# Two weight rings whose shifted blocks get columns of their own, and three small index tables that move

## The chip, the cores and the metric

The kernel runs on one core of one Trainium2 chip. The metric is the time of one execution in device microseconds (us). Before the change it was measured three times: 1804.21, 1804.41 and 1804.79 us, with a median of 1804.41 us.

## What is computed

The reference is a two-layer encoder trunk for one sequence of 256 tokens with 1024 features. Each layer is a token mixer and a channel mixer, each followed by a residual sum and a layer norm.

```python
for i in range(2):
    m = mla(x) if i == 0 else dsa(x)             # token mixer
    x = layernorm(alpha * x + m)
    x = layernorm(alpha * x + peer(x))           # channel mixer

# dsa (layer 1): h = x @ w_in gives q, k, v (8 heads of 128), index queries (8 heads of 64),
# one index key of 64 and 8 index weights for each token
score = sum_h w_idx[:, h] * relu(q_idx[:, h] @ k_idx.T)     # chunk-causal
sel   = top_k(score, 64)                                    # 64 keys for each query
o     = softmax(q @ k[sel].T * scale) @ v[sel];   m = o @ w_o

# peer: q = x @ w_q, two sub-keys for each head, top 16 x top 16 -> 16 of 16384 experts for each head
a = x @ w_down.T;  y = (gelu(a) * gate) @ w_up
```

The kernel computes all 16384 experts of a layer densely (128 blocks of 128 experts) and multiplies by a gate matrix that is zero for the experts that weren't chosen.

## The kernel before, in words

**The weights as a stream of blocks.** Nearly all weights pass through one object, `Stream` (L55 to L140). A block is 128 partitions by 1024 columns of float32. Its life has four steps. `_load` (L81) issues the DMA from HBM into one of four `raw` buffers, on the SP queue. `_split` (L99) lets ScalarE round it to a shorter format (`hi`, L106) and VectorE, at times GpSimd, subtract to get what is left (`lo`, L110 or L108). Then TensorE multiplies: each product is the sum of three, hi by hi, hi by lo and lo by hi, and all matmuls of the projections are issued in L264. `get()` (L114) hands out block i and, before it returns, issues the splits up to block i + 3 (`AHEAD`, L58) and the loads up to i + 6.

**The rings.** The `hi` and the `lo` parts have a buffer each (`ring`, L221): 4 slots of 1024 columns and 64 columns of padding. `parts(i)` (L75) places block i in slot i % 4. A block that TensorE streams as the moving operand (`moving=True` in L222 to L240) starts at the slot's first column; a block whose slices are loaded as stationary weights starts 16 columns later (`SKEW`). A shifted block therefore reaches 16 columns into the next slot. Between blocks of one kind this costs nothing, as all are shifted alike. Where the kind changes, a shifted block and the unshifted block in the next slot share 16 columns, and the instructions that write and read these columns are ordered by semaphores, in program order.

**The blocks by number**, in the order of the `add` calls: 0 to 5 `mla_h` and 6 to 12 `mla_qk` (shifted); 13 and 14 `mla_v`, 15 to 22 `mla_w_o`, 23 to 26 the first of `peer_q` (moving); 27 to 38 the rest of `peer_q` and 39 to 166 `down` (shifted); 167 to 294 `up` and 295 to 298 the first of `dsa_v` (moving); 299 to 302 `dsa_iq` and 303 `dsa_ik` (shifted); 304 to 307 the rest of `dsa_v` (moving); 308 to 323 `dsa_qk` (shifted); 324 to 331 `dsa_w_o` and 332 to 335 `peer_q` (moving); 336 to 347 `peer_q` and 348 to 475 `down` (shifted); 476 to 603 `up` (moving).

**The stage of the second half of `dsa_v`.** In `dsa()` the loop of L893 runs over the blocks 304 to 307, that is over c = 4 to 7, and for each over the two token tiles t. `rows` (L300) issues six matmuls of 512 columns for one block and one tile: two by each of hi, lo and hi again. Between them stand `weigh()` (L852: two small transposes of the index weights, PSUM tile `wi`) after block 305's first tile, and then `pick(2)`, which issues the index scores of two heads (PSUM tile `il`, L864). All of these matmuls are linked in program order by `pe()` (L254, from L891 on). The index key that `il` needs comes out of block 303 by a chain of copies and multiplications on ScalarE and VectorE: L845 and L846 (ScalarE), L847 to L849 (VectorE), L850 (ScalarE, the key's second copy) and L851 (ScalarE, the index weights). Behind the loop come the queries `q` from block 308 on.

Since `get()` splits three blocks ahead, `get()` for block 305 issues the split of block 308, the first shifted block, ahead of block 305's `rows`; block 306's call issues the split of 309, and block 307's that of 310.

**The start.** GpSimd writes `iota` (the numbers 0 to 127), VectorE casts it to `iota16` (L215) and, spread out, to `iotac` (L217), and GpSimd to `iota4` (L216). `first()` (L1198) begins with dummy matmuls (`busy`, L1204), which have `iota16` as weights and `iotac` as moving operand, until the first inputs are there.

**The order of instructions** that the program leaves open on ScalarE, VectorE and GpSimd is drawn up when the kernel is built, from a list of dependences and estimated times.

Of the kernel before, what the change touches and what calls it, by code (L numbers as in the profile page):

```python
# [10 lines left out]
F32 = mybir.dt.float32  # L11
F32R = mybir.dt.float32r
F16 = mybir.dt.float16
# [5 lines left out]
P = 128  # L19
T = 256  # L20
D = 1024
# [26 lines left out]
GSCALE = 2.0 ** 14  # L48
RING = 4
SKEW = 16  # L50
DSA_POOL = 3
MAGIC = 12582912.0


class Stream:  # L55
# [18 lines left out]

    def parts(self, i):  # L75

        skew = 0 if self.moving[i] else SKEW
        at = i % RING * D + skew
        return [ring[:, at : at + self.blocks[i][1]] for ring in (self.hi, self.lo)]

    def _load(self, upto):  # L81
# [89 lines left out]
def tile_trunk(ctx: ExitStack, tc: tile.TileContext, ins, out: bass.AP):  # L171
    nc = tc.nc
    def pool(name, bufs, **kw):
        return ctx.enter_context(tc.tile_pool(name=name, bufs=bufs, **kw))

    lead = pool("lead", 1)
    wide = pool("wide", 1)
    raws = pool("raws", 4)
    rings = pool("rings", 1)
    big = pool("big", 1)  # L180
    const = pool("const", 1)
# [9 lines left out]
    def ps(name):  # L191
        return psp.tile([P, 512], F32, tag="ps", name=name)
# [2 lines left out]
        return pyp.tile([P, 512], F32, tag=f"py{i}", name=name)  # L195

    ident = lead.tile([P, P], F32, tag="ident", name="ident")
    iota = const.tile([P, P], F32, tag="iota", name="iota")
    ones = lead.tile([P, 16], F32, tag="ones", name="ones")[:, 0:1]
    mhalf = lead.tile([P, 16], F32, tag="mhalf", name="mhalf")[:, 0:1]  # L200
    keep = [dram.tile([P, D], F32, tag=f"x{t}", name=f"x{t}") for t in range(2)]
    xh = wide.tile([P, NC, T], F32R, tag="xh", name="xh")
    xl = wide.tile([P, NC, T], F32R, tag="xl", name="xl")
    place16 = const.tile([P, 2, T], F16, tag="place16", name="place16")
    gate16 = const.tile([P, T], F16, tag="gate16", name="gate16")
    rest = const.tile([P, T], F32, tag="rest", name="rest")
    iota16 = lead.tile([P, P], F16, tag="iota16", name="iota16")
    iota4 = const.tile([P, P, 4], F16, tag="iota4", name="iota4")
    iotac = const.tile([P, CELLS, TOPK], F16, tag="iotac", name="iotac")
    arena = big.tile([P, 32768], F32, tag="arena", name="arena")  # L210
    A = arena.rearrange("p (b t) -> p b t", t=T)

    make_identity(nc, ident)
    nc.gpsimd.iota(iota, pattern=[[1, P]], base=0, channel_multiplier=0, allow_small_or_imprecise_dtypes=True)
    nc.vector.tensor_copy(iota16, iota)  # L215
    nc.gpsimd.tensor_copy(iota4, iota[:, :, None].to_broadcast([P, P, 4]))  # L216
    nc.vector.tensor_copy(iotac, iota[:, :CELLS, None].to_broadcast([P, CELLS, TOPK]))  # L217
    nc.vector.memset(ones, 1.0)
    nc.vector.memset(mhalf, -0.5)

    ring = [rings.tile([P, RING * D + 64], F32R, tag=k, name=k) for k in ("hi", "lo")]  # L221
    ws = Stream(nc, raws, *ring)  # L222
    ws.add(ins["mla_h"][0:6])
    ws.add(ins["mla_qk"])
# [38 lines left out]
    def mm(o, l, r, start, stop):  # L263
        return pe(lambda: nc.tensor.matmul(o, l, r, start=start, stop=stop, skip_group_check=True))  # L264
# [48 lines left out]
    def queue_of():  # L313

        last = {}

        def queue(engine, emit):
            with ExitStack() as order:
                if engine in last:
                    order.enter_context(tc.issue_after(last[engine]))  # L320
                ins = emit()
            last[engine] = ins.ins
            return ins

        return queue
# [492 lines left out]
    def dsa():  # L818
# [82 lines left out]
        for t in range(2):  # L901
            for n in range(2):
                nc.scalar.copy(v[:, t, n * 512 : (n + 1) * 512], v4[t][n])
        ws.share = DSA_POOL
        for h in range(0, HEADS, 2):
# [22 lines left out]
    def peer(li):  # L928
# [186 lines left out]
        def place(g4, done):  # L1115
# [8 lines left out]
            if done < P:  # L1124
                nc.scalar.mul(A[:, done:, tsl], pv[:, done:, :], 1.0 / GSCALE)
            if done:
                nc.vector.scalar_tensor_tensor(A[:, :done, tsl], pv[:, :done, :], 1.0 / GSCALE, A[:, :done, tsl],
                                               op0=ALU.mult, op1=ALU.mult)
# [3 lines left out]
        for b0 in range(0, NKEYS, 2):  # L1132
# [9 lines left out]
            if t0 < T:  # L1142
                nc.scalar.activation(A[:, b0 : b0 + 2, t0:], pv[:, :, t0:], AF.Gelu)
            if t0 > 0:
                nc.scalar.activation(pv[:, :, :t0], pv[:, :, :t0], AF.Gelu)
                nc.vector.tensor_tensor(A[:, b0 : b0 + 2, :t0], A[:, b0 : b0 + 2, :t0], pv[:, :, :t0], op=ALU.mult)
            while groups < prepared:
# [16 lines left out]
        def operand(k):  # L1164
            if k % 2 == 0 and k not in parts:
                a = A[:, k : k + 2, :]
                slot = slice(k % NC, k % NC + 2)
# [30 lines left out]
    def first(o):  # L1198

        queue = queue_of()  # L1200
        idle = ps("idle")
        some = iotac.rearrange("p c k -> p (c k)")

        def busy(n, w=P):  # L1204
            for _ in range(n):
                queue("pe", lambda: nc.tensor.matmul(idle[:, :w], iota16, some[:, :w], start=True, stop=True))

        def x_high(c, engine="act"):
            emit = nc.scalar.copy if engine == "act" else nc.vector.tensor_copy
            queue(engine, lambda: emit(xh[:, piece[c], :], xt[:, piece[c], :]))  # L1210

        def x_low(c, engine="dve"):
            eng = nc.vector if engine == "dve" else nc.gpsimd
            return queue(engine, lambda: eng.tensor_tensor(xl[:, piece[c], :], xt[:, piece[c], :],
                                                           xh[:, piece[c], :].bitcast(F32), op=ALU.subtract))

        def w_low(i):
            s = slice(512 * i, 512 * i + 512)
            queue("dve", lambda: nc.vector.tensor_tensor(lo0[:, s], raw0[:, s], hi0[:, s].bitcast(F32),
                                                         op=ALU.subtract))  # L1220

        def passes(w, x, *pieces):
            for c in pieces:
                for k in (2 * c, 2 * c + 1):
                    queue("pe", lambda: mm(o, w[:, k * P : (k + 1) * P], x[:, k, :], k == 0 and w is hi0 and x is xh,
                                           k == NC - 1 and w is lo0))

        queue("act", lambda: nc.scalar.copy(hi0, raw0))
        x_high(0, "dve")
        x_high(1)  # L1230
        x_low(0)
        x_low(1)
        x_high(2)
        pooled = x_low(2, "pool")
        x_high(3)
        w_low(0)
        x_low(3)
        w_low(1)
        busy(WARM, 512)
        passes(hi0, xh, 0, 1)  # L1240
        busy(2)
        passes(hi0, xl, 0)
        passes(hi0, xh, 2)
        passes(hi0, xl, 1)
        passes(hi0, xh, 3)
        busy(2)
        passes(lo0, xh, 0, 1)
        passes(hi0, xl, 2, 3)
        passes(lo0, xh, 2, 3)
        return pooled  # L1250
# [78 lines left out]
```

## Time and profile before

| | |
|---|---|
| median of three runs | 1804.41 us |
| the profiled execution's own time | 1804.73 us |
| its span in the profile | 1803.0 us |
| TensorE (PE) busy | 1786.7 us |
| VectorE (DVE) busy | 1338.9 us |
| ScalarE (ACT) busy | 1054.0 us |
| GpSimd (POOL) busy | 404.4 us |
| granted TensorE clock, mean | 0.998 |

PE is TensorE's matmuls, PEld its weight loads, SPq the queue that issues most DMAs. In a row of the timeline stand the start in us from the span's beginning, the duration in us, the engine, the line, the operation, the tile written and the tiles read, the count, and in square brackets the engine's idle time ahead of it with what ended it. In a row of the waits stand the instruction that waited and what it waited for, then the total in us, the number of waits and the longest one. In a row of the chain of waits stand the start, the duration and what ran. In a row of the windows stand, for a stretch, each engine's busy time and its count of instructions, then the granted TensorE clock, the DMA share and GB/s.

### The profile page before, as it was taken

The numbers are of one execution on the slowest core, as the hardware profiler recorded it, in microseconds if no ns is written. First come the engines' busy times: TensorE is split into PE (matmuls) and PEld (weight loads), VectorE is DVE, ScalarE is ACT, GpSimd is POOL, SyncE is SP. The second block draws the span as 40 slices with busy tenths as digits, with TensorE's granted clock in tenths as the row PEclk, the third lists the DMA queues.
The fourth block names the chain that finished last, engine by engine and source line by source line (L and its number), as shares of the span: only waits on it lengthen the run. The fifth ranks groups of instructions, "written<-read, shape, count | busy, mean of one in ns | idle before, by whom it ended". The sixth has DMA issues, their size and how long they took to land.

```text
span 1803.0 us, 32368 instructions
## 1 busy us (share of the span) xinstructions
PE 1786.7 (99%) x12495; PEld 1632.4 (91%) x12495; DVE 1338.9 (74%) x2320; ACT 1054.0 (58%) x1832; POOL 404.4 (22%) x287
## 2 busy tenths in 40 slices
PE   9999999999999999999989999999999999999998
PEld 8899999999998888888879899999999988888886
DVE  6688998888985555555679789997889865555555
ACT  6655545888864444444556554557888754444443
POOL 2012354555520000000013013543555400000000
PEclk9999999999999999999999999999999999999999
DMA  7555566444456666666646555655444575666653
GB/s 244 199 176 176 190 199 197 159 159 163 164 197 216 194 195 191 197 190 196 209 133 220 180 170 181 202 193 175 165 164 165 167 239 190 196 191 195 192 193 118
DMA packets 93468, 335.47 MB, mean 186 GB/s; under 512 B 10368, under 2 KB 11392, under 8 KB 93312
## 3 DMA queue, kind: packets, MB, share of 16 engines
q1 hardware_dynamic: 93024, 332.87, 56.4%
q8 instruction: 98, 1.61, 0.3%
q14 instruction: 58, 0.48, 0.1%
q10 hardware_dynamic: 288, 0.52, 0.1%
HBM read 329.16 MB, written 4.19 MB: 185 GB/s over the span
## 4 chain that ended last, share of the span: by engine, by line
PE 98%; DVE 1%; issue 1%; ACT 0%; DMA 0%; SPq 0%; DVEq 0%; POOLq 0%; POOL 0%; ACTq 0%
PE y L264 41%; PE d L264 39%; PE pq L264 4%; PE G L264 3%; PE q L264 3%; PE v L264 2%; PE qw L264 1%; PE s L264 1%; PE ps L264 1%; PE h L264 1%; PE qi L264 1%; PE o L264 1%; PE qn L264 0%; DMA arena<-in_xT 0%; PE kn L264 0%
## 5 line engine op out<-in xcount | busy, mean ns | idle before, releaser
L110 DVE TENSOR_TENSOR lo<-raw,hi 128x1024 fp32r<-128x1024 f32 (+1 forms) x557 | 750.7, 1349 | 291.2 <-ACT hi L106 289.5
L106 ACT CAST hi<-raw 128x1024 fp32r<-128x1024 f32 (+1 forms) x583 | 611.0, 1049 | 525.1 <-PE d L264 222.9
L264 PE MATMUL d<-xh,hi 128*128 128x256 f32 x2048 | 572.9, 280 | 0.0
L264 PE MATMUL d<-xh,lo 128*128 128x256 f32 x2048 | 566.8, 277 | 0.0
L264 PE MATMUL d<-xl,hi 128*128 128x256 f32 x2048 | 566.8, 277 | 0.0
L264 PEld LDWEIGHTS d<-xh,lo 128*128 128x128 f32 x2048 | 385.1, 188 | 0.0
L264 PEld LDWEIGHTS d<-xh,hi 128*128 128x128 f32 x2048 | 384.8, 188 | 0.0
L264 PEld LDWEIGHTS d<-xl,hi 128*128 128x128 f32 x2048 | 384.7, 188 | 0.0
L264 PE MATMUL y<-hi,xh 128*128 128x512 f32 x1088 | 337.8, 390 | 0.0
L264 PE MATMUL y<-lo,xh 128*128 128x512 f32 x1088 | 337.6, 389 | 0.0
L264 PE MATMUL y<-hi,xl 128*128 128x512 f32 x1088 | 337.4, 389 | 0.0
L1108 POOL TENSOR_TENSOR gate<-hot,gate 128x512 f16<-128x512 f16 x128 | 220.5, 1741 | 214.3 <-DVE hot L1106 214.3
L264 PEld LDWEIGHTS y<-lo,xh 128*128 128x128 f32 x1088 | 204.1, 188 | 42.7 <-DVE lo L110 0.3
L264 PEld LDWEIGHTS y<-hi,xl 128*128 128x128 f32 x1088 | 204.2, 188 | 42.4
L264 PEld LDWEIGHTS y<-hi,xh 128*128 128x128 f32 x1088 | 203.8, 188 | 42.0
L358 POOL TENSOR_TENSOR st<-st,mhalf 128x1 f32<-128x1 f32 x8 | 4.4, 552 | 800.6 <-DVE st L356 800.6
L1112 ACT ACTIVATE gate<-hot,rest 128x128 f16<-128x128 f16 x512 | 165.8, 411 | 1.1 <-DVE hot L1106 1.0
L1169 ACT CAST xh<-arena 128x512 fp32r<-128x512 f32 x128 | 79.7, 623 | 145.5 <-PE y L264 145.4
L1170 DVE TENSOR_TENSOR xl<-arena,xh 128x512 fp32r<-128x512 f32 x128 | 88.2, 691 | 73.8 <-ACT xh L1169 73.8
L108 POOL TENSOR_TENSOR lo<-raw,hi 128x1024 fp32r<-128x1024 f32 x26 | 62.8, 2414 | 223.8 <-ACT hi L106 223.8
L1106 DVE TENSOR_TENSOR hot<-iota,place 128x1024 f16<-128x1024 f16 x128 | 85.6, 709 | 32.4 <-PE G L264 32.2
L1030 POOL TENSOR_TENSOR arena<-arena 128x800 f32<-128x800 f16 x32 | 71.0, 2229 | 58.0 <-DVE arena L1027 58.0
(220 smaller groups left out, 1805.7 us busy)
## 6 DMA issues: line engine op xcount, KB each, us to landing
raw<-in_down SPq DMA_DIRECT2D x256, 512.0 KB, 3.3
raw<-in_up SPq DMA_DIRECT2D x256, 512.0 KB, 4.3
raw<-in_peer_q SPq DMA_DIRECT2D x24, 512.0 KB, 5.0
raw<-in_dsa_qk SPq DMA_DIRECT2D x16, 512.0 KB, 3.3
raw<-in_mla_w_o SPq DMA_DIRECT2D x8, 512.0 KB, 5.3
arena<-in_peer_q SPq DMA_DIRECT2D x8, 512.0 KB, 4.2
raw<-in_dsa_v SPq DMA_DIRECT2D x8, 512.0 KB, 4.4
raw<-in_dsa_w_o SPq DMA_DIRECT2D x8, 512.0 KB, 3.4
```

Source lines behind the costliest of these rows:

```text
L106: self.act(lambda: nc.scalar.copy(hi, raw))
L108: nc.gpsimd.tensor_tensor(lo, raw, hi.bitcast(F32), op=ALU.subtract)
L110: self.dve(lambda: nc.vector.tensor_tensor(lo, raw, hi.bitcast(F32), op=ALU.subtract))
L264: return pe(lambda: nc.tensor.matmul(o, l, r, start=start, stop=stop, skip_group_check=True))
L358: nc.gpsimd.tensor_tensor(st[:, 5:6], st[:, 4:5], mhalf, op=ALU.pow)
L1030: nc.gpsimd.tensor_tensor(o.rearrange("p k c -> p c k"), same, cell[t][:, h, :, None].to_broadcast([P, CELLS, TOPK]), op=ALU.mult)
L1106: nc.vector.tensor_tensor(hot, iota4[:, None].to_broadcast([P, 2, P, 4]), place16[:, :, None, four].to_broadcast([P, 2, P, 4]), op=ALU.is_ ...
L1108: nc.gpsimd.tensor_tensor(gate[:, 0], hot[:, 1].rearrange("p c j -> p j c"), gate16[:, four, None].to_broadcast([P, 4, P]), op=ALU.mult)
L1112: nc.scalar.mul(gate[:, 1, j, :], hot[:, 1, :, j], rest[:, t : t + 1])
L1169: nc.scalar.copy(hh, a)
L1170: nc.vector.tensor_tensor(al, a, hh.bitcast(F32), op=ALU.subtract)
```

## The change

The rings become two pairs of slots of 2112 columns each (`PAIR`), 4224 columns in place of 4160. In a pair, the even slot's block starts at column 0 (moving) or 16 (shifted), and the odd slot's block at 1088 (moving) or 1040 (shifted). The even slot thus ends at column 1040 at the latest and the odd one begins there at the earliest: no two slots share a column. In columns of the whole ring the shifted blocks start at 16, 1040, 2128 and 3152 in place of 16, 1040, 2064 and 3088, and the moving ones at 0, 1088, 2112 and 3200 in place of 0, 1024, 2048 and 3072.

For the 64 more columns in each ring other tables give way. `iota` becomes a piece of the big `arena` buffer (columns 30592 to 30719) that nothing else uses at that time; `iota16` and its cast are left out, and the dummy matmuls take the first 128 columns of `iotac` as weights in its place; `ones` moves from the pool `lead` to the pool `const`; `mhalf` gets 32 columns in place of 16. As a consequence most buffers move by some multiple of 64 bytes.

```diff
@@ -48,6 +48,9 @@
 GSCALE = 2.0 ** 14
 RING = 4
 SKEW = 16
+ODD = D + SKEW
+AFTER = 48
+PAIR = ODD + AFTER + D
 DSA_POOL = 3
 MAGIC = 12582912.0
 
@@ -74,8 +77,8 @@
 
     def parts(self, i):
 
-        skew = 0 if self.moving[i] else SKEW
-        at = i % RING * D + skew
+        pair, odd = divmod(i % RING, 2)
+        at = pair * PAIR + ((ODD + AFTER if self.moving[i] else ODD) if odd else (0 if self.moving[i] else SKEW))
         return [ring[:, at : at + self.blocks[i][1]] for ring in (self.hi, self.lo)]
 
     def _load(self, upto):
@@ -195,30 +198,28 @@
         return pyp.tile([P, 512], F32, tag=f"py{i}", name=name)
 
     ident = lead.tile([P, P], F32, tag="ident", name="ident")
-    iota = const.tile([P, P], F32, tag="iota", name="iota")
-    ones = lead.tile([P, 16], F32, tag="ones", name="ones")[:, 0:1]
-    mhalf = lead.tile([P, 16], F32, tag="mhalf", name="mhalf")[:, 0:1]
+    ones = const.tile([P, 16], F32, tag="ones", name="ones")[:, 0:1]
+    mhalf = lead.tile([P, 32], F32, tag="mhalf", name="mhalf")[:, 0:1]
     keep = [dram.tile([P, D], F32, tag=f"x{t}", name=f"x{t}") for t in range(2)]
     xh = wide.tile([P, NC, T], F32R, tag="xh", name="xh")
     xl = wide.tile([P, NC, T], F32R, tag="xl", name="xl")
     place16 = const.tile([P, 2, T], F16, tag="place16", name="place16")
     gate16 = const.tile([P, T], F16, tag="gate16", name="gate16")
     rest = const.tile([P, T], F32, tag="rest", name="rest")
-    iota16 = lead.tile([P, P], F16, tag="iota16", name="iota16")
     iota4 = const.tile([P, P, 4], F16, tag="iota4", name="iota4")
     iotac = const.tile([P, CELLS, TOPK], F16, tag="iotac", name="iotac")
     arena = big.tile([P, 32768], F32, tag="arena", name="arena")
     A = arena.rearrange("p (b t) -> p b t", t=T)
+    iota = arena[:, 30592:30720]
 
     make_identity(nc, ident)
     nc.gpsimd.iota(iota, pattern=[[1, P]], base=0, channel_multiplier=0, allow_small_or_imprecise_dtypes=True)
-    nc.vector.tensor_copy(iota16, iota)
     nc.gpsimd.tensor_copy(iota4, iota[:, :, None].to_broadcast([P, P, 4]))
     nc.vector.tensor_copy(iotac, iota[:, :CELLS, None].to_broadcast([P, CELLS, TOPK]))
     nc.vector.memset(ones, 1.0)
     nc.vector.memset(mhalf, -0.5)
 
-    ring = [rings.tile([P, RING * D + 64], F32R, tag=k, name=k) for k in ("hi", "lo")]
+    ring = [rings.tile([P, RING // 2 * PAIR], F32R, tag=k, name=k) for k in ("hi", "lo")]
     ws = Stream(nc, raws, *ring)
     ws.add(ins["mla_h"][0:6])
     ws.add(ins["mla_qk"])
@@ -1203,7 +1204,7 @@
 
         def busy(n, w=P):
             for _ in range(n):
-                queue("pe", lambda: nc.tensor.matmul(idle[:, :w], iota16, some[:, :w], start=True, stop=True))
+                queue("pe", lambda: nc.tensor.matmul(idle[:, :w], some[:, :P], some[:, :w], start=True, stop=True))
```

## The prediction

> **What bounds the kernel now.** I read the page first, for the engine that the end hangs on.
>
> ```profile
> span 1803.0 us, 32368 instructions
> ...
> PE 98%; DVE 1%; issue 1%; ACT 0%; DMA 0%; SPq 0%; DVEq 0%; POOLq 0%; POOL 0%; ACTq 0%
> ```
>
> The second row is the chain that ended last: 98% of it is TensorE. An edit that changes no matmul can only win what TensorE waits, or change the pace of its matmuls. So the second view is the list of TensorE's waits, over the whole span (total in us, times, longest).
>
> ```profile
> PE v L264 <- ACT hi L106: 2.7, 3, 1.2
> PE idle L1206 <- DVE iotac L217: 2.5, 1, 2.5
> PE v L264 <- DVE lo L110: 2.1, 3, 0.8
> PE qw L264 <- DVE xl L389: 0.6, 2, 0.3
> ```
>
> Waits for weights (`hi`, `lo`) occur six times, all in the matmuls of `v`, and nowhere else. The third view, the windows, shows where that is and what the other engines do there; the row behind it is the stretch that follows.
>
> ```profile
> 905.00:928.00 23.00, 18.29 (x80) 11.75 (x79) 11.01 (x23) 11.20 (x23) 1.29 (x1) 0.93 0.38 126
> 913.00:915.00 2.00, 2.00 (x6) 1.34 (x5) 0.00 (x0) 0.00 (x0) 0.00 (x0) 0.50 0.35 139
> 928.00:965.00 37.00, 37.00 (x304) 35.52 (x303) 34.97 (x74) 20.21 (x30) 12.00 (x7) 1.00 0.58 198
> ```
>
> From 905 to 928 TensorE is busy for 18.29 of 23.00 us, and for a part of that its granted clock is 0.50. From 928 on it is busy throughout. The fourth view is the timeline of that stretch, the loop over blocks 304 to 307.
>
> ```profile
> 905.45 0.63 PE L264 MATMUL v<-hi,xh 128*128 128x512 f32 x2
> ...
> 906.18 1.05 ACT L106 CAST hi<-raw 128x1024 fp32r<-128x1024 f32 x1
> ...
> 907.76 0.61 PE L264 MATMUL v<-hi,xl 128*128 128x512 f32 x2
> 908.46 1.04 ACT L106 CAST hi<-raw 128x1024 fp32r<-128x1024 f32 x1 [0.45 <-ACT arena L846]
> ...
> 909.55 0.73 PE L264 MATMUL v<-hi,xh 128*128 128x512 f32 x2 [1.18 <-ACT hi L106]
> 909.57 0.38 ACT L851 ACTIVATE arena<-ki 8x256 f32<-8x256 f32 x1
> 909.80 1.21 DVE L110 TENSOR_TENSOR lo<-raw,hi 128x1024 fp32r<-128x1024 f32 x1
> ...
> 911.06 0.73 PE L264 MATMUL v<-lo,xh 128*128 128x512 f32 x2 [0.78 <-DVE lo L110]
> 911.37 0.40 ACT L850 COPY arena<-arena 64x256 f32<-64x256 f32 x1 [1.42 <-DVE arena L849]
> ...
> 912.22 0.38 PE L267 MATMUL wi<-ident,arena 8*128 8x8 f32 x2
> ...
> 912.52 1.22 PE L264 MATMUL v<-hi,xh 128*128 128x512 f32 x2
> ...
> 915.38 0.53 PE L264 MATMUL il<-arena 64*128 64x128 f32 x4
> ...
> 916.63 0.73 PE L264 MATMUL v<-hi,xh 128*128 128x512 f32 x2 [0.72 <-ACT hi L106]
> ...
> 919.01 0.49 PE L264 MATMUL il<-arena 64*128 64x128 f32 x4
> ...
> 919.44 0.73 PE L264 MATMUL v<-hi,xh 128*128 128x512 f32 x2
> ...
> 921.02 0.49 PE L264 MATMUL il<-arena 64*128 64x128 f32 x4
> ...
> 922.27 0.50 PE L264 MATMUL v<-hi,xh 128*128 128x512 f32 x1 [0.76 <-ACT hi L106]
> ...
> 924.86 0.49 PE L264 MATMUL il<-arena 64*128 64x128 f32 x4
> ...
> 926.87 0.70 PE L264 MATMUL il<-arena 64*128 64x256 f32 x4
> ...
> 927.50 0.38 PE L264 MATMUL q<-xh,hi 128*128 128x256 f32 x1
> ```
>
> Block 304 runs from 905.45. Block 305 begins at 909.55, when a `hi` (908.46 to 909.50) has ended, and goes on at 911.06, when a `lo` (909.80 to 911.01) has ended. These are not block 305's own parts: the row at 906.18 is block 307's `hi` (it overwrites block 303, whose last matmul is just over), so the next one, at 908.46, is block 308's. Block 308 is shifted and sits in columns 16 to 1040, block 305 is not and begins at 1024; the split of 308 comes ahead of 305's matmuls in the program. They share 16 columns, so 305 waits for 308. In the same way 306 waits for 309 at 916.63 and 307 for 310 at 922.27. Each of these splits must in turn wait until the block four before it is used up, so TensorE, ScalarE and VectorE take turns instead of overlapping.
>
> **The change part by part.** *The rings.* No two slots share a column any more, so the three blocks start when the matmul ahead of them in the order is done. What each wait costs is the distance between two starts in the timeline, less the same distance where nothing waited. Undisturbed, a matmul of block 304 takes (907.76 - 905.45) / 10 = 0.231 us, so block 304 is through at 908.22; six matmuls up to the next score pair take 921.02 - 919.44 = 1.58; a score pair 919.44 - 919.01 = 0.43; four matmuls up to the transposes 912.22 - 911.06 = 1.16, of which 0.24 is the changeover.
>
> - 305 starts at 909.55 in place of 908.22: 1.33.
> - 305, first tile, 909.55 to 912.22 is 2.67 in place of 6 x 0.231 + 0.24 = 1.63: 1.04.
> - 305, second tile, 912.52 to 915.38 is 2.86 in place of 1.58: 1.28. Nothing is waited for here; this is the stretch at half clock (the windows' second row).
> - Scores to 306, 915.38 to 916.63 is 1.25 in place of 0.43: 0.82; then 916.63 to 919.01 is 2.38 in place of 1.58: 0.80.
> - Scores to 307, 921.02 to 922.27: 0.82 again; then 922.27 to 924.86 is 2.59 in place of 1.58: 1.01.
>
> That is 7.10 us. What is late next is the index key. The transposes `wi` read what L851 writes, which ends at 909.95; with the 0.05 that lie between the end at 909.50 and the matmul at 909.55, they start at 910.00, where 908.22 + 1.63 = 909.85 would be possible: 0.15 is lost. The first score pair would then come at 910.00 + 0.30 + 1.58 = 911.88 and needs L850, which ends at 911.77: just in time. L851 and L850 hang on block 303 and on the splits queued between them, that of 308 among them, and that split still follows block 304's end; so their times stay. The net is 7.10 - 0.15 = 6.95, and `q` starts at 920.55 in place of 927.50.
>
> Can the other engines do this? VectorE has 11.01 and ScalarE 11.20 us of work in that stretch, which fits into 23.00 - 6.95 = 16.05. Behind it VectorE is busy for 34.97 of 37.00 us, and this is where the gain could be given back. But that work (index scores, top-k, `lo` of the query blocks) is released by TensorE's own progress and moves ahead with it, so I count nothing. The loads of the query blocks are next:
>
> ```profile
> raw<-in_dsa_qk SPq DMA_DIRECT2D x16, 512.0 KB, 3.3
> ```
>
> A load is released by the `lo` four blocks before it, lands 3.3 us later and has four blocks' time until it is split. Block 309's `lo` moves ahead with TensorE, and so does the load of 313: nothing.
>
> *The other places where the kind changes.* From shifted to moving, blocks 12 and 13 and blocks 166 and 167 shared columns; 303 and 304, 323 and 324, 475 and 476 did not, as there the shifted block is in the last slot and reaches into the padding. From moving to shifted, a split waited for two blocks in place of one (28 and 29, 300 and 301, 336 to 338). All of these lie where the list of waits shows nothing for TensorE, so I count nothing; the bound for all of them together is the 0.6 us of the list's smallest row above, either way.
>
> *The start.* One cast goes ahead of `iotac`:
>
> ```profile
> 1.24 0.29 DVE L215 CAST iota<-iota 128x128 f16<-128x128 f32 x1 [0.35 <-POOL iota L214]
> ...
> 1.63 5.86 DMA arena<-in_xT
> ```
>
> The first row is VectorE's, the second the chain's first large piece. The dummy matmuls can begin up to 0.29 us earlier. But the first real matmuls wait for the input, which lands at 7.49; the cast is worth nothing as long as that DMA covers it, and 0.29 if it didn't. `ones` and `mhalf` are written in the same two instructions as before.
>
> *The places in memory.* No row shows the buffers at their new addresses. The nearest rows are those of the pace of matmuls: pieces of 48, in the chain of waits, of layer 0 (three) and layer 1 (the last).
>
> ```profile
> 336.26 5.71 PE d L264 x48
> ...
> 355.78 5.71 PE d L264 x48
> ...
> 524.19 5.71 PE d L264 x48
> ...
> 1300.86 5.52 PE d L264 x48
> ```
>
> The same 48 matmuls take 5.52 or 5.71. In layer 0 eleven pieces of 5.71 lie from 336.26 to 524.19, in layer 1 none. So 0.19 per piece is the price of an unknown cause, and 11 x 0.19 = 2.1 us what it moves in a layer, in either direction. I take zero, as the slow pieces come three pieces apart (19.52 us) while a piece is two blocks and the ring repeats after two pieces: the slot doesn't decide it. The 2.1 stays for the range.
>
> **The sum.** The profiled execution took 1804.73 us, 1.73 around its span of 1803.0, and stands 0.32 above the median of 1804.41. I take 6.95 off the median: 1797.5 us. A change of 0.2%, 3.6 us, is about what a measurement of this kernel can tell from none.
>
> **The rivals.** *The index key takes the wait's place.* The waits of the weight loads put 0.4 us of idle time before `wi` down to L850, not L851:
>
> ```profile
> PEld wi L267 <- ACT arena L850: 0.4, 1, 0.4
> ```
>
> If `wi` really waits for L850, it starts at 911.77 + 0.05 = 911.82 in place of 910.00, and the gain is 6.95 - 1.82 = 5.13: 1799.3. Against it: L850 is of another column range, and ahead of `wi` stand matmuls that run until then. 14 in 100.
>
> *The half clock stays.* When it sets in, TensorE has been idle in pieces of at most 1.18 us. If it isn't these pauses that bring it on, 1.28 of the gain stays away: 5.67, or 1798.7. [...] 8 in 100.
>
> *Nothing is left of it.* From 928 to 965 VectorE has 2.03 us free in 37.00. If its order there can't start earlier, TensorE waits for `lo` in the queries until the 6.95 are used up: 1804.4. Or the change doesn't do what it says, because the waits are kept for whole buffers and not for columns; against that stands the row at 906.18, a write into the ring while block 304 is multiplied from it. 8 in 100.
>
> *The matmuls get slower.* Slots 2 and 3 move by 64 columns, and the tables by odd steps. If the pace depends on that, pieces go from 5.52 to 5.71. The experts have 128 pieces in two layers, of which 117 aren't slow yet. From 6.95 / 0.19 = 37 more slow pieces on, the kernel is slower; with all 117 it is 22.2 - 6.95 = 15.3 slower, 1819.7. For it: such a second pace exists. Against it: the period of three. 7 in 100.
>
> **How the numbers follow.** The forecast has the remaining 63 in 100. Faster: 63 + 14 + 8 = 85; the same: 8; slower: 7. The forecast's own range is 1797.5 less and plus the 2.1 of the pace, 1795.4 to 1799.6. The rival of the index key, with the same 2.1 on top, ends at 1801.4, which also takes in a part of the gain given back. The range 1795.4 to 1801.4 leaves out the two last rivals, 15 in 100.
>
> **What the profile after would show.** Right: no waits of `v` for `hi` or `lo`; the `v` stage with a granted clock of 1.00 and some 15 us long from its first matmul to the first `q` (22.05 before); block 305 right behind 304; a wait of some 0.15 before `wi`; the experts' stages as long as before. Wrong: TensorE waits for `lo` in `q`; a longer idle time before `wi` or the first `il`; clock 0.50 in the stage all the same; more pieces of 5.71.

## The result, and the profile after

The changed kernel takes 1821.12 us (median of four runs, 1820.45 to 1821.57), the kernel before beside it 1804.31 us (four runs, 1803.92 to 1804.79). The ratio is 1.0093 [1.0075, 1.011]: slower by 16.8 us, where a gain of 6.95 was forecast. The profiled execution took 1821.57 us, with a span of 1819.8.

The page after, read first as before: the span and the chain that ended last.

```profile
span 1819.8 us, 32373 instructions
...
PE 98%; DVE 1%; issue 0%; ACT 0%; DMA 0%; SPq 0%; DVEq 0%; POOLq 0%; POOL 0%; ACTq 0%
```

TensorE is still the chain. The list of its waits (total in us, times, longest) is shorter than before:

```profile
PE idle L1207 <- DVE iotac L218: 1.9, 1, 1.9
PE h L265 <- ACT xh L1211: 0.9, 1, 0.9
...
PE wi L268 <- ACT arena L852: 0.3, 1, 0.3
```

No `v` waits for `hi` or `lo` any more; 4.8 us of such waits are gone. The windows over the `v` stage and the stretch behind it (columns as before):

```profile
916.00:932.00 16.00, 15.72 (x80) 11.12 (x79) 10.77 (x22) 11.12 (x23) 1.31 (x1) 1.00 0.51 176
932.00:969.00 37.00, 37.00 (x304) 35.52 (x303) 34.74 (x75) 20.19 (x31) 11.96 (x7) 1.00 0.57 199
```

TensorE is idle for 0.28 us of 16, its clock is 1.00, and the crowded stretch behind keeps it busy throughout. The timeline of the stage:

```profile
916.25 0.63 PE L265 MATMUL v<-hi,xh 128*128 128x512 f32 x2
...
919.01 0.62 PE L265 MATMUL v<-hi,xh 128*128 128x512 f32 x2
...
920.38 0.38 ACT L852 ACTIVATE arena<-ki 8x256 f32<-8x256 f32 x1
920.80 0.29 PE L268 MATMUL wi<-ident,arena 8*128 8x8 f32 x2 [0.28 <-ACT arena L852]
...
922.18 0.41 ACT L851 COPY arena<-arena 64x256 f32<-64x256 f32 x1 [1.43 <-DVE arena L850]
922.61 0.51 PE L265 MATMUL il<-arena 64*128 64x128 f32 x4
...
931.29 0.39 PE L265 MATMUL q<-xh,hi 128*128 128x256 f32 x1
```

From the first `v` to the first `q` it takes 931.29 - 916.25 = 15.04 us in place of 22.05. So the stage gained what it was to gain, and something else cost 24 us. The chain of waits shows where, if one follows the start of the same piece in both kernels (us from the span's start). In it `pq` are the query products of the channel mixer, `qwT` the transposes of its first query rows, `ps` the scores against the sub-keys, `d` the products with `down`, `G` groups of sixteen small matmuls that build a part of the gate matrix, and `y` the products with `up`.

| piece | before | after | difference so far |
|---|---|---|---|
| layer 0, first query transposes `qwT` | 108.41 | 108.24 | -0.17 |
| layer 0, the 1366 matmuls of `d` | 149.42 | 150.44 | +1.02 |
| layer 0, gate transposes `gT` | 304.25 | 311.33 | +7.08 |
| layer 0, first `y` | 529.90 | 540.69 | +10.79 |
| layer 1, first transposes `xt` | 878.09 | 888.88 | +10.79 |
| layer 1, first `q` behind the `v` stage | 927.57 | 931.36 | +3.79 |
| layer 1, the 1366 matmuls of `d` | 1068.89 | 1073.90 | +5.01 |
| layer 1, gate transposes `gT` | 1223.72 | 1234.78 | +11.06 |
| layer 1, first `y` | 1447.31 | 1464.15 | +16.84 |

The last difference is that of the spans, 1819.8 - 1803.0 = 16.8. The `y` stage, over 340 us in each layer, doesn't change at all (348.19 us in layer 0 in both). The loss lies in the `pq` and `d` matmuls of both layers: 1.19 + 6.06 + 3.71 in layer 0 and 1.22 + 6.05 + 5.78 in layer 1. Nothing waits there. The matmuls themselves run at another pace. The chain of before, from the first query product's last matmuls on, and its long piece:

```profile
105.82 2.59 PE pq L264 x22
...
108.41 0.44 PE qwT L958 x4
108.85 0.82 PE pq L264 x7
109.67 0.44 PE qwT L958 x4
110.10 2.17 PE pq L264 x19
...
149.42 154.83 PE d L264 x1366
```

The chain after:

```profile
105.64 2.59 PE pq L265 x22
...
108.24 0.87 PE qwT L959 x8
109.11 3.07 PE pq L265 x26
...
150.44 160.89 PE d L265 x1366
...
343.70 5.71 PE d L265 x48
...
350.33 5.71 PE d L265 x48
```

Two things are to be seen. First, 1366 matmuls take 154.83 us, 113.3 ns each, before, and 160.89 us, 117.8 ns each, after: the same two paces as in the pieces of 48 (5.52 and 5.71 us). Of the 33 pieces between the `G` groups, 31 are slow in each layer, where 11 and none were slow before: 51 more. The slow pace is not new, either: in both kernels the last 22 matmuls ahead of the transposes take 2.59 us (117.7 ns each), and the 216 of `q` in layer 1 take 25.64 us (118.7). In before the pace is fast from the transposes to the end of the long piece; in after it stays slow. Second, TensorE's own order is not the same. The eight transposes of the query rows (`turn()`, called at the start of the first query pair) stood four and four, seven matmuls of the second product apart; now they stand together. Apart from the dummy matmuls' weights, this is the only difference in the sequence of TensorE's matmuls. So TensorE belongs to the engines whose order is partly left open to the build: `turn()` is only told to come behind the first product (`tc.issue_after`). Ahead of it, on ScalarE, the casts `hi` and the copies of the rows that `turn()` reads change places too:

```profile
104.05 1.05 ACT L106 CAST hi<-arena 128x1024 fp32r<-128x1024 f32 x1 [1.44 <-PE qw L264]
105.01 0.58 ACT L952 COPY arena<-qw 128x512 f32<-128x512 f32 x1
105.67 1.05 ACT L106 CAST hi<-arena 128x1024 fp32r<-128x1024 f32 x1
106.62 0.58 ACT L952 COPY arena<-qw 128x512 f32<-128x512 f32 x1
```

The same part of the timeline after:

```profile
104.10 1.05 ACT L109 CAST hi<-arena 128x1024 fp32r<-128x1024 f32 x1 [0.72 <-ACT hi L109]
105.06 1.21 ACT L953 COPY arena<-qw 128x512 f32<-128x512 f32 x2
```

Here the ring turns from moving to shifted blocks, and the split of block 28 or 29 has one dependence less. The order drawn up when the kernel is built came out differently for it; that this one dependence did it is read from the two programs and was not tried by itself. That the ring brings the new order, and not the moved tables, is shown by the kernel with the tables alone, below: its order on TensorE is before's.

### The profile page after: what moved, and what is told of

It is laid out like the page before. It is cut to its first block, busy times and chain, and to the rows that moved or that the text cites. A ratio compares the mean times of both kernels' runs of the same rounds, so it can differ in the third digit from the quotient of the medians.

```text
span 1819.8 us, 32373 instructions
## 1 busy us (share of the span) xinstructions
PE 1807.5 (99%) x12495; PEld 1655.1 (91%) x12495; DVE 1339.2 (74%) x2319; ACT 1053.5 (58%) x1832; POOL 401.1 (22%) x287
## 4 chain that ended last, share of the span: by engine, by line
PE 98%; DVE 1%; issue 0%; ACT 0%; DMA 0%; SPq 0%; DVEq 0%; POOLq 0%; POOL 0%; ACTq 0%
PE y L265 40%; PE d L265 40%; PE pq L265 4%; PE G L265 3%; PE q L265 2%; PE v L265 1%; PE qw L265 1%; PE s L265 1%; PE h L265 1%; PE ps L265 1%; PE qi L265 1%; PE o L265 1%; PE qn L265 0%; DMA arena<-in_xT 0%; PE kn L265 0%
## 5 line engine op out<-in xcount | busy, mean ns | idle before, releaser
L265 PE MATMUL d<-xh,hi 128*128 128x256 f32 x2048 | 581.0, 284 | 0.0
L265 PE MATMUL d<-xh,lo 128*128 128x256 f32 x2048 | 575.3, 281 | 0.0
L265 PE MATMUL d<-xl,hi 128*128 128x256 f32 x2048 | 575.0, 281 | 0.0
L265 PEld LDWEIGHTS d<-xl,hi 128*128 128x128 f32 x2048 | 392.8, 192 | 0.0
```

## The experiments

Two causes are possible for the slower pace. *Order*: the transposes that now stand together. *Places*: the buffers' new addresses. The rival of both is that the ring's new slots themselves, from which every slow matmul reads, set the pace. Each comparison below is with runs of the kernel before on the same chip, whose median lies between 1803.36 and 1804.87 us; differences between two experiments carry this uncertainty of some 1 us. Where no interval is given, there is one run.

**Order back, places and rings as changed.** Two kernels fix TensorE's order by hand: the second group stands behind the second product's matmul number `TURN_AT`, 7 as in before, or 6.

```diff
+TURN_AT = 7
...
+        def second(first, o):
+            put = queue_of()
+            put("pe", lambda: first)
+            turn(put, 0)
+            (wh, wl), k = ws.get(), 0
...
+                    if k == TURN_AT:
+                        turn(put, 1)
+                    put("pe", lambda: mm(o, w[:, s], x[:, c, :], k == 0, k == 3 * NC - 1))
...
-                with tc.issue_after(first.ins):
-                    turn()
+                second(first, pv[:, 1, :])
```

> The changed kernel, with one thing put back: in the experts' first query pair the second group of four transposes stands again behind the seventh matmul of the second product, as in the kernel before, and not beside the first group. The memory stays as changed. Theory O (the pace of the 256-column matmuls is a state that is set where other matmuls interrupt the stream, so the place of the transposes decides): 113.3 ns a matmul in pq and in the long d piece of both layers, in place of 117.8; 2 x (1366 + some 240) x 4.5 ns = 14.4 us less, about 1807, and some us less still (1800) if the pieces between the G matmuls follow. Theory A (the addresses set the pace): 117.8 stays, 1821.

> As the first kernel of this call, but the second group of transposes stands behind the sixth matmul, between two triples of hi by hi, hi by lo and lo by hi, and not behind the first of a triple. Theory O, if the place in the triple decides: 117.8 ns, about 1821. Theory O, if it is enough that the two groups stand apart: 113.3 and about 1807 or less. Theory A: 117.8 and 1821.

Measured: 1806.47 us with 7 (10 runs, against 1803.36; ratio 1.0015 [1.0006, 1.0025]) and 1806.43 with 6. The chain of waits with 7:

```profile
149.38 154.83 PE d L266 x1366
...
323.32 5.71 PE d L266 x48
```

The long piece is back at 113.3 ns, and some 14 us are back: 1821.12 - 1806.47 = 14.65, or 16.81 - 3.11 = 13.7 if each is taken beside its own runs of before; the trace's price for `pq` and the long `d` is 14.5. The pieces of 48 stay slow, 31 and 31. So the order accounts for `pq` and the long `d`, and for nothing of the pieces. Six or seven makes no difference.

**New order alone.** The kernel before, with `TURN_AT = 0`: both groups together, everything else as it was.

> The kernel before, with one thing changed: both groups of transposes stand together ahead of the second product, as in the changed kernel. Memory and rings as before. Theory O: pq and the long d piece at 117.8 ns in both layers, about 1804.3 + 14.4 = 1819, up to 1825 if the pieces between the G matmuls follow. Theory A: 113.3 ns and 1804.3, as before.

Measured: 1820.4 us (4 runs), ratio 1.0091 [1.0074, 1.0108].

```profile
107.62 0.87 PE qwT L958 x8
108.50 3.07 PE pq L265 x26
...
149.82 160.89 PE d L265 x1366
```

The kernel before loses 17 us by this alone, in its old rings and at its old addresses: 14.5 for the pace of `pq` and `d` and 13 more slow pieces (12 in each layer). The new ring isn't needed for it.

**New places alone.** The changed kernel's tables with before's overlapping ring; its order on TensorE comes out as before's.

```diff
-        pair, odd = divmod(i % RING, 2)
-        at = pair * PAIR + ((ODD + AFTER if self.moving[i] else ODD) if odd else (0 if self.moving[i] else SKEW))
+        skew = 0 if self.moving[i] else SKEW
+        at = i % RING * D + skew
...
-    ring = [rings.tile([P, RING // 2 * PAIR], F32R, tag=k, name=k) for k in ("hi", "lo")]
+    ring = [rings.tile([P, RING * D + 64], F32R, tag=k, name=k) for k in ("hi", "lo")]
```

> The changed kernel's tables (iota in the arena, no iota16, ones in the other pool) with the rings of before, whose blocks overlap; most buffers move, and the matmuls stand in the order of before. Theory O: the paces of before, 1804. Theory A, if the moved buffers decide: 117.8 ns in pq and d, 1819 or more. Theory A, if only the new slots of the rings decide: 1804 too.

Measured: 1813.17 us (ratio 1.0049 [1.0033, 1.0066]). The long piece runs at 113.3 ns, the waits of `v` are as before (2.7 and 2.0 us), and of the pieces 31 and 31 are slow. This is 9.8 us more than before, for 51 more slow pieces: 0.19 each, the price the prediction had. The tables do this without the new ring. The opposite, the new ring without moved tables, wasn't tried, as the tables had made room for it.

**Which of the places.** The buffers whose contents the matmuls of `G` multiply, just ahead of each piece of 48, are `hot` and `gate`. The built programs place them, in bytes of a partition, at 220864 and 224960 before (192 above a multiple of 256) and at 220672 and 224768 after (0 above it). The next four kernels have the same instructions in the same order as the one with `TURN_AT = 7`, and only move buffers: the first three by widening `ones`, so that everything behind it moves by 192, 64 or 128 bytes, the fourth by widening `iotac`, so that only what lies behind `iotac` moves (by 192), `hot` and `gate` among it.

```diff
-    ones = const.tile([P, 16], F32, tag="ones", name="ones")[:, 0:1]
+    ones = const.tile([P, 64], F32, tag="ones", name="ones")[:, 0:1]
...
-    iotac = const.tile([P, CELLS, TOPK], F16, tag="iotac", name="iotac")
+    iotac = const.tile([P, CELLS + 6, TOPK], F16, tag="iotac", name="iotac")[:, :CELLS, :]
```

(`[P, 32]` and `[P, 48]` in place of `[P, 64]` for the second and third; counted from before's places, the three are shifts by 0, 128 and 64 bytes.)

> The changed kernel with the transposes put back as in e1, and with ones 64 columns wide instead of 16: all that lies behind the arena (place16, gate16, rest, iota4, iotac, the small tiles, hot and gate) comes to stand at exactly its address of before; xh, xl and hi stay 256 bytes lower, the arena 256 higher, and no instruction moves. Theory B (the addresses of what lies behind the arena set the pace of the pieces of 48 matmuls between the groups of G): slow pieces as in the kernel before, 11 in layer 0 and none in layer 1, in place of 31 and 31; 51 x 0.2 = 10 us less than e1, about 1796 beside 1803.4 for the kernel before. Theory C (xh, xl, hi or the arena decide): 31 and 31 slow pieces and 1806, as e1.

> As e1, with ones 32 columns wide: all behind the arena stands 64 bytes higher than in e1, 128 lower than in the kernel before; hot and gate start 64 bytes behind a multiple of 128, as before. Theory B with a period of 128 bytes: few slow pieces, about 1796. Theory B without it (only the old address is good): 31 and 31, 1806.

> As e1, with ones 48 columns wide: all behind the arena stands 128 bytes higher than in e1, 64 lower than in the kernel before; hot and gate start at a multiple of 128, as in the changed kernel. Theory B with a period of 128 bytes: 31 and 31 slow pieces, 1806. If the pace followed the distance to the old address, fewer than in e1.

> As e1, with iotac six rows longer: place16, gate16, rest, iota4 and iotac stay where the change put them, and only the small tiles, hot and gate are back at their addresses of before (hot and gate 64 bytes behind a multiple of 128). Theory B1 (hot and gate, which TensorE reads in G, decide): 11 and 0 slow pieces, about 1796. Theory B2 (the tables of VectorE, GpSimd and ScalarE decide): 31 and 31, about 1806.

Measured, beside 1804.65 us of the kernel before (the first row is the earlier measurement, beside 1803.36):

| `hot` and `gate`, bytes above a multiple of 256 | us | slow pieces of 33, layer 0 and 1 |
|---|---|---|
| 0 (as changed, `TURN_AT = 7`) | 1806.47 | 31, 31 |
| 64 | 1807.89 | 30, 30 |
| 128 | 1795.71 | 0, 0 |
| 192 (`ones` widened) | 1797.53, ratio 0.9959 [0.9945, 0.9973] | 12, 0 |
| 192 (`iotac` widened) | 1796.46 | 0, 0 |

At 0 and at 64 nearly all pieces are slow, at 128 none, at 192 none to twelve. The last row says that it is enough to move what lies behind `iotac`. The row above it is the change's ring with before's order and before's places of the small tables, with 12 and 0 slow pieces where before has 11 and 0: 7.1 us less than before, 1797.53, and 1797.5 was the forecast. That the two agree so closely is in part luck: in its profile the first query transposes come 0.7 us earlier than in before, which the forecast didn't count. All of this stands with the new ring's slots, so the rival, the slots, falls.

**`hot` or `gate`.** One more pool, for `gate`, and 128 bytes between: first `gate` alone at 128, then `hot` alone (there `ones` is widened as well, which moves all that lies between them and it).

```diff
+    gap = pool("gap", 1)
+    ohu = pool("ohu", 2)
...
-            gate = ohp.tile([P, 2, 4, P], F16, tag="U", name="gate")
+            gate = ohu.tile([P, 2, 4, P], F16, tag="U", name="gate")
```

> As e1 (hot and gate start at a multiple of 256 bytes, 31 and 31 slow pieces), but gate, the moving operand of G, starts 128 bytes behind a multiple of 256, as in e7; hot, the stationary one, stays. Theory B-gate: no slow pieces, about 1796. Theory B-hot: 31 and 31 slow pieces, about 1806.

> As e7 (hot and gate 128 bytes behind a multiple of 256, no slow pieces), but gate starts at a multiple of 256 again; hot stays at its place of e7. Theory B-gate: 31 and 31 slow pieces, about 1806. Theory B-hot: none, about 1796.

Measured: 1806.77 us, 31 and 31 slow, with `gate` moved; 1801.07 us, 17 and 17 slow, with `hot` moved (1804.87 before). The chain of the latter:

```profile
316.39 5.50 PE d L269 x48
...
322.83 5.71 PE d L269 x48
...
329.46 5.50 PE d L269 x48
...
335.89 5.71 PE d L269 x48
```

Every other piece is slow. `hot` and `gate` have two buffers each, which alternate in the same way; that this is the reason isn't shown. `gate` moved without `hot` changes nothing; with `hot` at 128, `gate` at 0 or at 128 makes 17 or no slow pieces in each layer, so `gate` counts too. For `hot` the runs are less clean: in each run that moves it the small tiles between `iotac` and `hot` move along, and that these have no part isn't shown.

**Both mended, and one alone.** The changed kernel with the order of before and `ones` of 48 columns (`hot` and `gate` at 128); and the changed kernel with `ones` of 48 columns only, its own order kept.

> The kernel of e7 once more, timed in rounds: the changed kernel with the transposes at their old place and hot and gate 128 bytes higher. With both causes mended it should beat the kernel before by the 6.95 us of the stage of v and 11 slow pieces x 0.2 = 2.2 us: some 9 us, 0.995 of the kernel before.

> The changed kernel with ones 48 columns wide and nothing else: hot and gate as in e7, the two groups of transposes side by side as in the changed kernel. If the two causes add up: no slow pieces of 48, but 117.8 ns in pq and the long d piece of both layers, so about 1795.7 + 14.5 = 1810, 11 us less than the changed kernel.

Measured: 1794.39 us with both mended (5 runs, 1794.17 to 1795.62; 0.9943 [0.993, 0.9957] of before), faster than both kernels. This is 10.5 us less than before, where some 9 were expected; in the profile 7.0 lie in the stage of `v`, 2.9 in the pieces and 0.5 ahead of the first query transposes. With the places alone 1809.31 us, 1.0026 [1.0015, 1.0036]: no piece slow, the long piece slow:

```profile
150.51 160.89 PE d L265 x1366
...
324.07 5.51 PE d L265 x48
```

The two causes add up: 1809.31 - 1794.39 = 14.9 for the order, and 1821.12 - 1809.31 = 11.8 for the places (62 slow pieces at 0.19; 16.81 - 4.44 = 12.4 beside their own runs of before).

**What about the order decides.** Four kernels, all on the mended one, to tell three theories apart: a *row* of eight transposes brings the slow pace; the groups' *distance* does; or it is the *place* of the last group inside the second product, the last interruption setting the pace.

```diff
-TURN_AT = 7
+TURN_AT = 1
```

> The mended kernel with only one matmul between the two groups of four transposes. If a stretch of eight in a row is what brings the slow pace (row), 113.3 ns in pq and the long d and about 1795.5 us. If the distance between the groups matters (distance: at least some six matmuls), 117.8 ns and about 1810 us (14.5 more). If only the second group's coming after the start of the product matters (place), 113.3 ns.

For the second and third, `turn(put, 0)` leaves its place ahead of the product, and both groups stand behind the seventh matmul, or one behind the seventh and one behind the fourteenth.

```diff
-            turn(put, 0)
...
-                    if k == TURN_AT:
-                        turn(put, 1)
+                    if k in (TURN_AT, 2 * TURN_AT):
+                        turn(put, k // TURN_AT - 1)
```

> The mended kernel with both groups together, but behind the second product's seventh matmul. Row: eight stand in a row, so 117.8 ns and about 1810 us. Distance: 117.8 ns as well. Place: the last transposes come behind the start of the product, so 113.3 ns and about 1795.5 us.

> The mended kernel with the first group of four behind the second product's seventh matmul and the second group behind its fourteenth. Row, distance and place all expect 113.3 ns and about 1795.5 us; 117.8 ns would mean that a group of four must stand at the border of the two products.

In the fourth both groups stand together ahead of the product, and the second group's four transposes are done once more behind the seventh matmul.

```diff
             turn(put, 0)
+            p = ps("qwT1")
+            four(put, p, 1)
...
                     if k == TURN_AT:
-                        turn(put, 1)
+                        turn(put, 1, p)
```

> The mended kernel with both groups together ahead of the second product, as in the changed kernel, and the second group's four transposes done once more behind the seventh matmul (twice the same work, 0.4 us more in each layer). If the last interruption sets the pace and the stretch of eight ahead of it doesn't matter (last, and place), 113.3 ns and about 1796.5 us. If eight in a row set a pace that lasts (row, kept), 117.8 ns and about 1811 us.

Measured, beside 1804.2 us of the kernel before: 1808.94 with one matmul between, 1801.13 with eight behind the seventh, 1793.27 with both groups inside, 1795.73 with four more. The first has no eight in a row and is slow (117.8 ns) in both layers: the *row* falls. The second is the surprise. Its chain in layer 0 and in layer 1:

```profile
108.62 0.87 PE qwT L959 x8
109.50 2.51 PE pq L266 x22
...
148.81 154.83 PE d L266 x1366
...
1018.20 0.87 PE qwT L959 x8
1019.08 2.59 PE pq L266 x22
...
1059.57 160.89 PE d L266 x1366
```

The same instructions in the same order, fast in one layer and slow in the other: so neither *distance* nor *place* decides either. The fourth shows when the pace changes:

```profile
109.08 0.87 PE qwT L958 x8
109.95 0.83 PE pq L266 x7
110.78 0.44 PE qwT L958 x4
111.22 2.00 PE pq L266 x17
113.22 0.89 PE ps L266 x8
114.11 0.12 PE pq L266
114.23 0.89 PE ps L266 x8
115.12 5.34 PE pq L266 x47
```

Behind the last transposes it is still slow (2.00 / 17 = 117.6 ns); it turns fast behind the second group of scores `ps` (5.34 / 47 = 113.6 ns), with one matmul since the group ahead. All three theories as put have fallen. What all runs agree with is this: between two interruptions (transposes, scores, `G` groups) the pace doesn't change; with each interruption it can change, and it shows in the first step behind it. These are the steps in ns from the start of the first matmul behind an interruption to the start of the second, from the trace:

```
kernel, layer                 interruptions in order: step, pace behind it
before, 0                     4 T: 207 fast   4 T: 207 fast   ps: 206 fast   all later ps: 206 fast
after, 0                      8 T: 201 slow   ps: 201 slow    all later ps: 201 slow
one matmul between, 0         4 T: 204 (one matmul)   4 T: 201 slow   ps: 200 slow
eight behind seventh, 0       8 T: 202, then 122 and 115: fast   ps: 206 fast
eight behind seventh, 1       8 T: 201 slow   ps: 201 slow
both groups inside, 0         4 T: 202 slow   4 T: 206 fast   ps: 206   ps: 205 fast
four more, 0                  8 T: 200 slow   4 T: 203 slow   ps: 200   ps: 206 fast
192 (`ones` widened), 0       4 T: 201 slow   4 T: 204, then 126 and 127: fast   ps: 206 fast
```

In these stretches a first step of 205 to 207 ns is followed by the fast pace, one of 200 to 204 by the slow one, except one of 202 and one of 204, whose next steps are longer than elsewhere. The last row is a kernel with before's order on TensorE, and yet its first four transposes leave the pace slow: this order, too, doesn't always bring the fast pace at once. What the order does decide in these profiles is the long piece. In all 22 layers with the groups six or seven matmuls apart (11 profiles) it is fast, in all 8 with eight transposes together ahead of the product, or one matmul between the groups, and no more transposes behind (4 profiles), it is slow. Behind the `G` groups the step doesn't tell it: 203 ns comes ahead of fast pieces in before and of slow ones after. What the interruption leaves lasts until the next one, and in the long piece of `d` there is none for 1366 matmuls (154.83 or 160.89 us).

What remains open: what in TensorE holds the pace, why it comes out slow behind `hot` and `gate` at 0 or 64, and why at 192 none, 12 in one layer or 12 in both are slow. TensorE's weight loads run beside its matmuls (from 150 to 300 us both are busy for 150.00 of 150.00 us, before and after), and one of them goes with the pace: in the slow pace one weight load of each triple takes 192 ns, the others 188, as these rows of the page after have it (line, tile, count, busy us, mean ns).

```profile
L265 PEld LDWEIGHTS d<-xl,hi 128*128 128x128 f32 x2048 | 392.8, 192 | 0.0
L265 PEld LDWEIGHTS d<-xh,hi 128*128 128x128 f32 x2048 | 384.7, 188 | 0.0
L265 PEld LDWEIGHTS d<-xh,lo 128*128 128x128 f32 x2048 | 384.6, 188 | 0.0
```

In the long piece of layer 0 (155 to 300 us) the `xl,hi` loads take 192 ns on average in after and 188 in before. So spacing and load change together (117.8 and 192 ns, 113.3 and 188 ns); which of them brings the other isn't shown.

## Why the prediction was wrong, point by point

**The rings: right.** A net gain of 6.95 us was forecast and 7.00 came (10.79 - 3.79). All six waits are gone. The forecast wait before `wi` is there, on the instruction that was named (the index weights, L852 now): 0.28 us in place of 0.15. The first scores were to come just in time: L851 (the key's second copy) ends at 922.59, they start at 922.61.

**The index key: the rival fell.** `wi` waits for the index weights, not for the key's second copy.

**The half clock: the rival fell.** It went with the waits. Of the 18 profiles, the three that keep the waits of `v` (before, the new order alone, the tables alone) have a stretch at 0.50 in that stage, for 3.41 or 10.24 us, though the longest wait of `v` in them is 1.2 us; the fifteen others have none there. Whether the waits bring it on every time isn't shown: of the thirteen executions of before beside the mended kernel, three have a mean granted clock of 0.999 (the fastest 1802.47 us), which is also that of four of the mended kernel's five, and the others 0.996 to 0.998. So the 1.28 us counted for it may not be a gain in every execution.

**Nothing given back: right.** The stretch behind the stage has TensorE busy for 37.00 of 37.00 us, and the gain is carried on to the next query products.

**The start: near in size by luck.** 0.29 at most was named, and the first query transposes come 0.17 earlier. But this is a net of other things. The profile after has a granted clock of 0.92 over its first 10 us (1.00 before) and waits 1.5 us for `xh` in `h` (0.2 before); against that, 24 matmuls of `krope` take 2.72 us in place of 2.83, and 36 of `qr` 4.10 in place of 4.27. The mended kernel, with the full clock there, is 0.5 ahead. What the left-out cast alone is worth isn't shown.

**The other places where the kind changes: the step that failed first.** The prediction counted nothing for them, with a bound of 0.6 us, since TensorE waits for nothing there. But the new ring also changed the order that the build draws up. By the runs the two groups of transposes moved together cost some 14 to 15 us (13.7 and 14.65 from the changed kernel against the same with the old order, 14.9 at the mended places). The premise was in the first paragraph: "An edit that changes no matmul" could only act on waits or on the pace. The edit changed no matmul, but it changed where eight transposes stand, and with them the pace of 1656 matmuls in each layer: 1656 x 4.5 ns x 2 = 14.9.

**The places in memory: the step that failed second.** The term was taken as zero with a bound of 2.1; it was 9.5 in the trace (3.71 + 5.78). The price per piece was right (0.19), the number was not: 51 more pieces in place of at most 11. The reason given, that slow pieces come three apart and so "the slot doesn't decide it" (the last of the eleven comes two after the one ahead), was right about the ring's slot and was then used for all buffers. What decides it is where the buffers behind `iotac` lie, `gate` and, by all that is shown, `hot`, and these moved too.

**The rival "The matmuls get slower" was the case.** Its break-even of 37 more slow pieces was passed with 51. Its worst case, 1819.7 us, is only 1.4 us off: its 117 pieces are all the blocks of `down` not yet slow, taken two by two, so the long piece of `d` is among them, though only 66 pieces stand between `G` groups. The query products are not in it, and it was given 7 in 100. That the query products and the long piece could lose their pace was to be had from the rows of before: 154.83 / 1366 = 113.3 ns in the long piece against 2.59 / 22 = 117.7 in the first query product. And both signs were open, as the mended kernel shows: the eleven slow pieces of before are gone in it too.

## What to carry to other kernels

Where TensorE is busy throughout, ask not only for waits: look whether the same matmuls run at more than one pace, and price each long stretch at both before calling an edit neutral. An edit that removes a dependence or moves a buffer can change the order or the place of things it doesn't name; compare the order of the two programs engine by engine, and try the other order and some offsets of the small buffers (here 64 bytes) as cheap variants. A change that loses may hold its gain all the same: the ring's 7.0 us were there in the slower kernel.

## What of the hardware was not expected

- In these traces a stream of 256-column matmuls in three terms runs at 113.3 or at 117.8 ns each, and keeps its pace over 1366 matmuls (154.83 or 160.89 us) until something interrupts it.
- The place of buffers matters for matmuls that don't read them: with `hot` and `gate`, which the `G` matmuls just ahead read, at 0 or 64 bytes above a multiple of 256, 30 or 31 of 33 pieces are slow, at 128 none, at 192 none to twelve. The 512-column matmuls of `y` didn't care: 389 or 390 ns in the page after, and the stage is as long as before (348.19 us in layer 0 in both).
- The same kernel can have the half clock at its start in one execution and not in another: the mended kernel had 0.94 over the first 10 us in one profile and 1.00 in the other.
